# The cosine product of the rotation, made by VectorE instead of GpSimd, in a two-layer trunk on one core

## The chip, the cores and the metric

The kernel runs on one core of a Trainium2 chip. The metric is the device time of one execution in microseconds; the time before is the median of three runs. The profile is that of one further execution.

## What is computed

Two layers of a transformer trunk over 512 latent tokens (x) and 256 context tokens (ctx), width 1024, all in float32. Each layer projects the normed tokens into queries, keys and values of four groups of heads (differential, windowed, latent, grouped), attends, projects back (`w_out`), and then runs a gated feed-forward network with a short convolution. The queries and keys of the 512 latent tokens are rotated by position before they are used; this is the part that the change touches:

```
def apply_axial_rope(x, cos, sin):
    ...
    x1, x2 = xr[..., 0, :], xr[..., 1, :]
    ...
    out = jnp.stack([x1 * c - x2 * s, x2 * c + x1 * s], axis=-2)
    return out.reshape(B, S, H, d)
```

## The kernel before

Features lie on the 128 partitions, tokens along the free dimension. TensorE works in pairs of rounded floats: each float32 operand is split into a high part (ScalarE rounds it, line 249) and a low part (value minus high part, line 250, on VectorE or GpSimd), and a product is three matmuls (lines 263 to 265).

A layer has four stages. In the trace, layer 0's mixing stage lies at 55 to 470 us and layer 1's at about 1190 to 1510 us; the feed-forward network and the output projection fill the rest. In a mixing stage the kernel walks through a hand-written string of steps (`ORDER`): projections (`DQ0`, `DK0`, ...), values (`Vd`, `Vs`), heads of attention (`d0` to `d3`, `s0`, `g0`, ...), and the three steps of the latent group (`mla`). A scheduler then orders the instructions of every engine by its own estimate of their times, so that projections, softmaxes and value products of several steps interleave. When one instruction moves to another engine, the scheduler lays the whole stage out anew.

A projected tile is called `p` (or `qr` in the latent group): 128 rows by 768 tokens, of which the first 512 are rotated. The rotation (`rope`) is called 12 times a layer: ten projections, once on half a tile (64 rows), and once for `qr`. It makes two products with the sines into a scratch tile `u`, with the halves of the partitions exchanged (lines 635 and 636, 64 rows each, VectorE), one product with the cosines in place on `p` (line 642, 128 rows by 512), and a sum (line 643, VectorE). The rotated tile is split by `hilo` into `f` (ScalarE's line 249, then GpSimd's line 250), written to DRAM (`sc`, line 771) and read back by heads as an operand `op` (lines 777, 785, 792), all from SP's DMA queue, in order. The scores `s` (line 820) need that operand.

Softmax in these stages takes a maximum on VectorE (lines 828 and 834, from PSUM), the exponential on ScalarE (837), a reciprocal on VectorE (841), and a scaling on GpSimd (862, 865), with a subtraction on VectorE for the differential heads (863). The probabilities `P` are transposed on TensorE (889) into `tp`, split into `pth` (ScalarE) and `ptl` (VectorE, line 250), and multiplied with the values into `po` (896). GpSimd also makes the low parts of the weights, `wl` (line 250).

Of the kernel before, what the change touches and what calls it, by code (L numbers as in the profile page):

```python
# [14 lines left out]
ALU = mybir.AluOpType  # L15
# [7 lines left out]
S = 512  # L23
# [81 lines left out]
def _tables():  # L105
    pos = np.arange(S)
    row = (pos // 64).astype(np.float32)
    col = (pos % 64).astype(np.float32)

    def make(dim):  # L110
        n = dim // 4
        inv = (np.float32(10000.0) ** (-np.arange(n, dtype=np.float32) / np.float32(n))).astype(np.float32)
        r = np.arange(64) % (2 * n)
        a, i = r // n, r % n
        ang = np.where(a[:, None] == 0, row[None], col[None]).astype(np.float32) * inv[i][:, None]
        c, s = np.cos(ang).astype(np.float32), np.sin(ang).astype(np.float32)
        return np.concatenate([c, c], 0), np.concatenate([s, -s], 0)

    c64, s64 = make(64)
    c32, s32 = make(32)  # L120
    rope = np.ascontiguousarray(np.stack([c64, s64, c32, s32], 1))
    m = np.full((P, 7, P), NEG, np.float32)
    q = np.arange(P)[:, None]
    k = np.arange(P)[None]
    m[:, 3] = 0.0
    m[:, 2] = np.where(k >= q, 0.0, NEG)
    m[:, 4] = np.where(k <= q, 0.0, NEG)
    mask = np.ascontiguousarray(m[:, 1:6]).reshape(P, 5 * P)
    sel = np.zeros((P, 4), np.float32)
    r = np.arange(P)  # L130
    for h in range(2):
        sel[:, h] = (r % 64) // 32 == h
        sel[:, 2 + h] = r // 64 == h
    return rope, mask, sel
# [101 lines left out]
class Prog:  # L236
# [393 lines left out]
    def rope(self, p, tab, mp, rows=None):  # L630
        nc = self.nc
        ct, st = (self.ropet[:, 0], self.ropet[:, 1]) if tab == 64 else (self.ropet[:, 2], self.ropet[:, 3])
        u = self.mq.tile([P, T], F32, tag="u", bufs=1, name="u")[:, :S]
        if rows is None:
            nc.vector.tensor_tensor(out=u[0:64], in0=p[64:128, :S], in1=st[64:128], op=ALU.mult)
            nc.vector.tensor_tensor(out=u[64:128], in0=p[0:64, :S], in1=st[0:64], op=ALU.mult)
            a, b = 0, 128
        else:
            nc.vector.tensor_tensor(out=u[64:96], in0=p[96:128, :S], in1=st[96:128], op=ALU.mult)
            nc.vector.scalar_tensor_tensor(out=u[96:128], in0=p[64:96, :S], scalar=-1.0, in1=st[64:96], op0=ALU.mult, op1=ALU.mult)  # L640
            a, b = 64, 128
        nc.gpsimd.tensor_tensor(out=p[a:b, :S], in0=p[a:b, :S], in1=ct[a:b], op=ALU.mult)
        nc.vector.tensor_tensor(out=p[a:b, :S], in0=p[a:b, :S], in1=u[a:b], op=ALU.add)

    def hilo(self, p, n, mp, a=0, b=P):
# [656 lines left out]
```

## Time and profile before

| what | value |
|---|---|
| median of three runs | 1975.7 us (1970.12 to 1979.73) |
| profiled execution, its own time | 1973.07 us |
| span in its trace | 1971.3 us |
| PE busy | 1805.3 us, 92% of the span |
| DVE busy | 1135.2 us, 58% |
| ACT busy | 905.0 us, 46% |
| POOL busy | 838.5 us, 43% |

PE is TensorE's matmuls, DVE is VectorE, ACT is ScalarE, POOL is GpSimd, SP the engine that issues the DMAs. Busy shares are averages over stages that differ; the rows further down take the mixing stages apart. In a timeline row the first number is the start, the second the time it took, and the bracket at the end gives how long the engine sat idle before it and which instruction ended that.

### The profile page before, as it was taken

To read this page: it belongs to the slowest core of one execution; us is meant where nothing else is said; L and a number is where in the kernel's file an instruction comes from. 1 tells how busy PE (TensorE), PEld (TensorE's weight loads), DVE (VectorE), ACT (ScalarE), POOL (GpSimd) and SP (SyncE) were. 2 spreads that over 40 slices of the span, in tenths; PEclk is the share of its full clock that TensorE was granted. 3 is DMA by queue.
4 is the path that set the end of the run, shared out by engine and by line. 5 is a ranking of instruction groups with operands and counts; after the bars stand their busy time and mean duration, and the time that the engine had idled before them with its cause. 6 is when DMAs were issued, how large, how long until landed. Compare 5 with 4: busy or idle time off the path is not lost. (4 is left out here: it accounts for less than half of the span.)

```text
span 1971.3 us, 26510 instructions
## 1 busy us (share of the span) xinstructions
PE 1805.3 (92%) x9834; PEld 1530.0 (78%) x9834; DVE 1135.2 (58%) x2119; ACT 905.0 (46%) x1597; POOL 838.5 (43%) x559
## 2 busy tenths in 40 slices
PE   6889899898988899999999977888899899999997
PEld 3878778776877788888888866777777788888885
DVE  5466877875769755454432675776786632323235
ACT  5455567875542323231313363554787444333332
POOL 1363534543234334242424434544454145545553
PEclk8999899999998999999999998989999989999999
DMA  8663452544345324242312136524253323222322
GB/s 313 185 191 108 113 172 84 174 110 148 112 173 190 118 75 161 85 150 107 118 43 86 53 130 156 128 65 119 65 150 118 119 86 98 96 96 96 107 86 85
DMA packets 76160, 239.97 MB, mean 122 GB/s; under 512 B 11136, under 2 KB 12672, under 8 KB 73216
## 3 DMA queue, kind: packets, MB, share of 16 engines
q1 hardware_dynamic: 76032, 238.28, 38.5%
q8 instruction: 78, 1.28, 0.3%
q14 instruction: 50, 0.41, 0.1%
HBM read 201.94 MB, written 36.31 MB: 121 GB/s over the span
## 5 line engine op out<-in xcount | busy, mean ns | idle before, releaser
L250 POOL TENSOR_TENSOR wl<-wr,wh 128x1024 fp32r<-128x1024 f32 (+1 forms) x178 | 440.2, 2482 | 499.7 <-ACT wh L249 478.6
L249 ACT ACTIVATE wh<-wr 128x1024 fp32r<-128x1024 f32 (+1 forms) x186 | 193.2, 1049 | 383.7 <-PE up L264 182.5
L1222 DVE SCALAR_TENSOR_TENSOR ut<-up,pc,ut 128x769 f32<-128x769 f32 (+1 forms) x84 | 74.1, 883 | 333.6 <-ACT ut L1221 333.6
L263 PE MATMUL up<-hx,wh 128*128 128x512 f32 x672 | 262.8, 391 | 0.0
L264 PE MATMUL up<-hx,wh 128*128 128x512 f32 x672 | 262.5, 391 | 0.0
L265 PE MATMUL up<-hx,wl 128*128 128x512 f32 x672 | 262.2, 390 | 0.0
L820 PE MATMUL s<-op 128*128 128x256 f32 (+4 forms) x648 | 160.2, 358 | 34.2 <-ACT P L837 18.3
L250 DVE TENSOR_TENSOR ptl<-tp,pth 128x512 fp32r<-128x512 f32 (+1 forms) x208 | 136.2, 663 | 40.7 <-ACT pth L249 39.6
L820 PEld LDWEIGHTS s<-op 128*128 128x128 f32 (+1 forms) x648 | 110.8, 198 | 56.8 <-ACT P L837 28.3
L265 PEld LDWEIGHTS up<-hx,wl 128*128 128x128 f32 x672 | 126.4, 188 | 27.1
L263 PEld LDWEIGHTS up<-hx,wh 128*128 128x128 f32 x672 | 126.5, 188 | 25.6
L264 PEld LDWEIGHTS up<-hx,wh 128*128 128x128 f32 x672 | 126.5, 188 | 25.1
L1127 PE MATMUL dn<-wh,gh 128*128 128x512 f32 x440 | 140.3, 398 | 4.6 <-ACT gh L249 4.2
L865 POOL TENSOR_SCALAR P<-P,st 128x768 f32<-128x768 f32 (+2 forms) x120 | 95.9, 801 | 114.1 <-DVE st L841 84.5
L1127 PE MATMUL dn<-wl,gh 128*128 128x512 f32 x440 | 139.3, 396 | 0.0
L889 PE MATMUL tp<-ident,P 128*128 128x128 f32 x800 | 127.9, 280 | 12.2 <-DVE P L863 6.8
L1127 PE MATMUL dn<-wh,gl 128*128 128x512 f32 x440 | 138.0, 398 | 0.0
L249 ACT ACTIVATE pth<-tp 128x512 fp32r<-128x512 f32 (+1 forms) x208 | 116.6, 576 | 38.2 <-PE tp L889 36.7
L837 ACT ACTIVATE P<-s,st 128x768 f32<-128x768 f32 (+2 forms) x120 | 94.1, 786 | 79.2 <-DVE st L828 35.0
L497 DVE SCALAR_TENSOR_TENSOR wm<-wm,cb 128x1024 f32<-128x1024 f32 x56 | 107.1, 1925 | 31.4 <-DMA wm<-wmod 31.1
L828 DVE TENSOR_REDUCE st<-s 128x1 f32<-128x768 f32 (+2 forms) x120 | 95.6, 808 | 50.7 <-PE s L820 49.7
L896 PE MATMUL po<-ptl,vt 128*128 128x256 f32 x400 | 112.3, 303 | 13.2 <-DVE ptl L250 13.2
(286 smaller groups left out, 4326.5 us busy)
## 6 DMA issues: line engine op xcount, KB each, us to landing
wr<-wup SPq DMA_DIRECT2D x88, 512.0 KB, 3.8
wm<-wmod SPq DMA_DIRECT2D x56, 512.0 KB, 5.0
wr<-wdn SPq DMA_DIRECT2D x44, 512.0 KB, 3.8
op<-sc SPq DMA_DIRECT2D x36, 384.0 KB, 5.4
wr<-win SPq DMA_DIRECT2D x26, 512.0 KB, 4.3
wk<-wmk SPq DMA_DIRECT2D x12, 1024.0 KB, 6.9
op<-sc SPq DMA_DIRECT2D x60, 192.0 KB, 5.6
wm<-wm SPq DMA_DIRECT2D x8, 1024.0 KB, 9.4
```

The source lines that it names most:

```text
L249: self.nc.scalar.activation(out=hi, in_=src, func=AF.Copy)
L250: eng.tensor_tensor(out=lo, in0=src, in1=hi.bitcast(F32), op=ALU.subtract)
L263: mm(ps, lh, rh, start=first, stop=False)
L264: mm(ps, lh, rl, start=False, stop=False)
L265: mm(ps, ll, rh, start=False, stop=last)
L497: nc.vector.scalar_tensor_tensor(out=j, in0=raw, scalar=1.0, in1=cb[v], op0=ALU.mult, op1=ALU.mult, accum_out=self.mods[l][:, ch, f, v:v + 1])
L820: nc.tensor.matmul(full[:, o:o + w], q[:rows, qcol:qcol + P], k[:rows, c0:c0 + w], start=i == 0, stop=i == len(passes) - 1 and not msk)
L828: nc.vector.tensor_reduce(out=nm, in_=ps[:, :nk], axis=AX.X, op=ALU.max, negate=True)
L865: nc.gpsimd.tensor_scalar(out=a[:, :nk], in0=a[:, :nk], scalar1=ra, scalar2=1.0, op0=ALU.mult, op1=ALU.mult)
L889: nc.tensor.transpose(tp[:, a * 256 + j * P:a * 256 + (j + 1) * P], ptile[j][:, pos[kt]:pos[kt] + P], self.ident)
L896: nc.tensor.matmul(po[:, :256], vw, t[:, a * 256:(a + 1) * 256], start=n == 0, stop=n == total - 1)
L1127: mm(ps[:, c], a, b[:, c], start=first and i == 0, stop=last and i == 2)
```

## The change

The product with the cosines is issued to VectorE's queue, where the other three instructions of the rotation stand.

```
             a, b = 64, 128
-        nc.gpsimd.tensor_tensor(out=p[a:b, :S], in0=p[a:b, :S], in1=ct[a:b], op=ALU.mult)
+        nc.vector.tensor_tensor(out=p[a:b, :S], in0=p[a:b, :S], in1=ct[a:b], op=ALU.mult)
         nc.vector.tensor_tensor(out=p[a:b, :S], in0=p[a:b, :S], in1=u[a:b], op=ALU.add)
```

The scheduler's order changes on every engine in both mixing stages. On VectorE, at the start of layer 0's mixing stage (the rotation of `DQ0`; `wl` is the low part of a weight tile), a piece of the difference:

```order
 L635 TENSOR_TENSOR u<-p,ropet 64x512
 L636 TENSOR_TENSOR u<-p,ropet 64x512
+L642 TENSOR_TENSOR p<-p,ropet 128x512
 L250 TENSOR_TENSOR wl<-wr,wh 128x1024
 L643 TENSOR_TENSOR p<-p,u 128x512
```

The product now stands between the second product with the sines and the weight's low part. Of the 24 products six stand directly behind the second product with the sines (three of them the first three of layer 1); the other 18 have one to four other instructions in between.

On VectorE, later in layer 1's mixing stage, the sixth rotation of that layer (at 1259 us in the trace), before:

```order
L635 TENSOR_TENSOR u<-p,ropet 64x512
L636 TENSOR_TENSOR u<-p,ropet 64x512
L828 TENSOR_REDUCE st<-s 128x1
L841 RECIPROCAL st<-st 128x1
L250 TENSOR_TENSOR ptl<-tp,pth 128x512
L841 RECIPROCAL st<-st 128x1
L643 TENSOR_TENSOR p<-p,u 128x512
```

and of the change:

```order
L635 TENSOR_TENSOR u<-p,ropet 64x512
L636 TENSOR_TENSOR u<-p,ropet 64x512
L828 TENSOR_REDUCE st<-s 128x1 x2
L642 TENSOR_TENSOR p<-p,ropet 128x512
L250 TENSOR_TENSOR ptl<-tp,pth 128x512 x2
L841 RECIPROCAL st<-st 128x1
L643 TENSOR_TENSOR p<-p,u 128x512
```

The product now stands ahead of the low parts of the probabilities (`ptl`).

On SP's queue, at the start of layer 0's mixing stage (the writes of `DQ0`'s and `DK0`'s rotated tiles to `sc`, and the reads of the first operands):

```order
 L771 DMA sc<-f 16x2x768 x8
-L777 DMA op<-sc 32x2x768 x3
-L771 DMA sc<-f 16x2x768 x8
-L777 DMA op<-sc 32x2x768 x5
+L777 DMA op<-sc 32x2x768
+L771 DMA sc<-f 16x2x768 x8
+L777 DMA op<-sc 32x2x768 x7
 L511 DMA wk<-wmk 128x2048 x2
```

Two of the first operand's reads moved from ahead of `DK0`'s eight writes to behind them.

## Rows read from the trace of the kernel before

**Rows 1.** The page's busy times: engine, us, share of the span, instructions.
```profile
PE 1805.3 (92%) x9834; PEld 1530.0 (78%) x9834; DVE 1135.2 (58%) x2119; ACT 905.0 (46%) x1597; POOL 838.5 (43%) x559
```

**Rows 2.** Busy times by window, the two mixing stages; columns in the first line.
```profile
core 0: us, PE busy (x) PEld busy (x) DVE busy (x) ACT busy (x) POOL busy (x), PEclk, DMA share, GB/s
...
55.00:470.00 415.00, 376.23 (x2459) 326.50 (x2459) 294.83 (x655) 264.30 (x582) 196.13 (x193) 0.96 0.49 141
...
1190.00:1510.00 320.00, 274.75 (x1692) 240.83 (x1691) 229.65 (x479) 194.69 (x404) 155.01 (x137) 0.95 0.43 110
```

**Rows 3.** Waits of PE in layer 0's mixing stage: total us, times, longest.
```profile
PE s L820 <- DMA op<-sc: 2.8, 1, 2.8
```

**Rows 4.** Waits of PE in layer 1's mixing stage.
```profile
PE s L820 <- DMA op<-sc: 12.8, 3, 7.8
PE po L896 <- DVE ptl L250: 9.5, 10, 2.8
PE tp L889 <- DVE P L863: 3.7, 3, 2.7
```

**Rows 5.** Line 642: ns min/median/max; below, who waited for it, us and times.
```profile
L642 POOL TENSOR_TENSOR p<-p,ropet x22: 1260/1288/2027, 58.8 to 1377.9; 128x512 f32<-128x512 f32 x20, 64x512 f32<-64x512 f32 x2
...
  DVE p L643: 7.9, 7
```

**Rows 6.** Line 636 alone by window: length, busy us (instructions), clock, DMA.
```profile
55.00:470.00 415.00, 7.54 (x11) 0.96 0.49 141
1190.00:1510.00 320.00, 8.18 (x10) 0.95 0.43 110
```

**Rows 7.** Line 635 alone, the same windows and columns.
```profile
55.00:470.00 415.00, 10.28 (x11) 0.96 0.49 141
1190.00:1510.00 320.00, 13.69 (x10) 0.95 0.43 110
```

**Rows 8.** Timeline, a rotation at the start of layer 1's mixing stage.
```profile
1190.83 2.68 DVE L635 TENSOR_TENSOR u<-p,ropet 64x512 f32<-64x512 f32 x1 [2.25 <-ACT p L625]
1193.51 0.69 DVE L636 TENSOR_TENSOR u<-p,ropet 64x512 f32<-64x512 f32 x1
1194.35 1.29 POOL L642 TENSOR_TENSOR p<-p,ropet 128x512 f32<-128x512 f32 x1 [1.39 <-DVE u L636]
1195.67 0.69 DVE L643 TENSOR_TENSOR p<-p,u 128x512 f32<-128x512 f32 x1 [1.47 <-POOL p L642]
```

**Rows 9.** Timeline of DVE: first, largest and last beside line 642, two without it.
```profile
59.39 1.76 DVE L250 TENSOR_TENSOR wl<-wr,wh 128x1024 fp32r<-128x1024 f32 x1 [0.73 <-ACT wh L249]
...
61.68 1.21 DVE L250 TENSOR_TENSOR wl<-wr,wh 128x1024 fp32r<-128x1024 f32 x1
...
223.34 0.15 DVE L840 TENSOR_TENSOR st<-st 128x1 f32<-128x1 f32 x1
...
243.78 1.27 DVE L283 TENSOR_SCALAR rs_y<-rs_v 128x12 int32<-128x12 int32 x1
...
1378.57 0.56 DVE L840 TENSOR_TENSOR st<-st 128x1 f32<-128x1 f32 x1
```

**Rows 10.** Timeline of PE: first, largest and last wait for VectorE behind a rotation.
```profile
130.59 0.63 PE L889 MATMUL tp<-ident,P 128*128 128x128 f32 x4 [1.08 <-DVE ptl L250]
...
1335.71 0.39 PE L896 MATMUL po<-ptl,vt 128*128 128x256 f32 x1 [2.81 <-DVE ptl L250]
...
1379.52 0.39 PE L896 MATMUL po<-ptl,vt 128*128 128x256 f32 x1 [1.66 <-DVE ptl L250]
```

**Rows 11.** Timeline of SP's DMA issues and of PE, starts of both mixing stages.
```profile
70.83 3.59 SPq L771 DMA_DIRECT2D sc<-f  x8
74.46 2.32 SPq L777 DMA_DIRECT2D op<-sc  x5
...
1203.56 3.25 SPq L777 DMA_DIRECT2D op<-sc  x7
...
1213.47 0.77 PE L820 MATMUL s<-op 128*128 128x512 f32 x1 [7.84 <-DMA op<-sc]
```

**Rows 12.** Timeline of PE, a wait for an operand later in layer 1.
```profile
1347.97 0.59 PE L820 MATMUL s<-op 128*128 128x384 f32 x2 [1.39 <-DMA op<-sc]
```

## Prediction

> **What bounds the kernel now.** I began with the page's busy times: TensorE is busy for 92% of the span and no other engine for more than 58% [rows 1]. So only what lets TensorE stand still can move the time much. The change acts in the two mixing stages alone, so I next took the windows of those stages. TensorE is busy for 376.2 of 415 us in layer 0's and 274.8 of 320 us in layer 1's [rows 2]; it stands still for 38.8 and 45.2 us, 84 us in both. VectorE is busy for 294.8 of 415 us (71%) and 229.7 of 320 us (72%), GpSimd for 47% and 48%. The reader should see that work goes from an engine with more room to one with less, and that neither is the bound. The lists of what TensorE waited for name two things that a rotation can touch: operands that come late from DRAM, 2.8 us in layer 0 and 12.8 us in layer 1 [rows 3, 4], and VectorE, of which layer 1's largest entries are 9.5 us for `ptl` and 3.7 us for `P` [rows 4].
>
> **What is removed.** 24 products leave GpSimd, 1.29 us each in the median [rows 5], 31 us. GpSimd had room, so this by itself gives nothing. Two side effects do. VectorE stood idle for the product in 7 of the 24 rotations, 7.9 us in all [rows 5]. And some VectorE instructions were stretched while GpSimd made the product: a weight's low part took 1.76 us beside it and 1.21 us without it, a 128x1 sum 0.56 us and elsewhere 0.15 us, and one small scalar operation 1.27 us [rows 9]. I found eight that are clearly stretched, by 0.4 to 1.1 us, 5.4 us together (first, largest and last stand in the rows).
>
> **What is added.** 24 products on VectorE. The trace has none of this operation on VectorE, so I bound it by its neighbours in the same rotation, which have the same free length. The lower is line 636, which stands right behind another VectorE product: 7.54 + 8.18 us for 21, mean 0.75 us [rows 6], so 18.0 us for 24. The upper is line 635, which often starts while GpSimd is busy: 10.28 + 13.69 us for 21, mean 1.14 us [rows 7], so 27.4 us. I take 0.75, since every new product has the two products with the sines close ahead, as line 636 has line 635. VectorE's account over both stages is then 18.0 added, 5.4 given back in stretched instructions and 7.9 in idle time: 4.7 us more, of 735 us.
>
> **Which of it lies on the path.** I looked behind each rotation for the next wait of TensorE that VectorE ends. There are eight places (1.08 us at 130 us, 2.81 at 1335, 1.66 at 1379 are the first, the largest and the last [rows 10]), and I compared them with the new order. At two of the eight the awaited instruction now stands ahead of the product, so nothing is added. At six the product stands ahead of it, as in the sixth rotation of layer 1 shown above: 6 × 0.75 = 4.5 us more. At two of these six a stretched instruction stood on the way, 0.6 and 0.4 us, which goes: 1.0 us less. Net 3.5 us. At the other rotations TensorE has other matmuls queued that hide 0.75 us; without that cover the remaining 18 × 0.75 = 13.5 us would come on top.
>
> **The operands.** At the start of layer 1 the rotation is bare: the second product with the sines ends at 1194.20, the sum starts at 1195.67, 1.47 us later [rows 8]. With the product on VectorE in between this is about 0.75, so the tile is ready 0.7 us earlier, then the split, the writes and the reads, for which TensorE waits 7.84 us at 1213 [rows 11]. I take 0.8 us off for the two rotations ahead of it, at least 0 if the transfers and not the rotation set the pace. In layer 0 the tile is also 0.7 us earlier, but the new queue of SP puts two reads of the first operand behind `DK0`'s writes; at the old pace of five reads in 2.32 us [rows 11] they hold the awaited ones up by 2 × 0.46 = 0.9 us. I take 0. Later in layer 1 a wait of 1.39 us at 1348 [rows 12] hangs on a rotation in which `ptl` twice comes first and the product then follows in series, where GpSimd used to work beside it: 0.6 us more. Sum for operands: −0.8 + 0 + 0.6 = −0.2 us.
>
> **A rule weighed against this.** In the trace a VectorE product of 64x512 takes 2.68 us behind a busy GpSimd and 0.69 us right after [rows 8]. The Trainium skill (SBUF — State Buffer, Who interferes with whom) says that a VectorE instruction with two SBUF inputs contends with a GpSimd instruction that reads SBUF, and that whichever starts first has the shared port for its whole length. The stretched first product agrees. By that rule the new product could be held as line 635 is; that is the first rival, priced from rows below.
>
> **Sum.** 3.5 − 0.2 = 3.3 us on the profiled execution's own 1973.07 us gives 1976.4 us. That execution lies 2.6 us below the median of the three runs, 1975.7; moved by as much, the forecast is 1979 us, 0.17% slower than before. About 0.5% (9.9 us) is what a measurement of this kernel can tell from no change, so I call this no change: within 1965.8 to 1985.6 us.
>
> **Rivals.**
> *VectorE is held up (slower).* Each new product starts while GpSimd is making a low part, and takes 1.14 us; VectorE works in order, so all behind it waits. Then 27.4 − 5.4 − 7.9 = 14.1 us more if all of it reaches TensorE: 1990 us. It decides from about 70% of that (9.9 us) on. For it: 18 of the 24 products have other instructions between them and the products with the sines, so a GpSimd instruction can slip in; VectorE is at 71%. Against: TensorE waited for `ptl` and `P` only 13.2 us in layer 1 [rows 4].
> *The rotation is on the path (faster).* The step from the second product to the sum shrinks from 1.47 to 0.75, 0.72 us [rows 6, 8], and 24 × 0.72 = 17 us is the most that this can give: 1958 us. With 16 of the 24 on the path it is 11.5 us: 1964 us. It decides from 14 on. For it: the 15.6 us of waits for operands [rows 3, 4]. Against: VectorE idled for the product in only seven rotations [rows 5].
> *The new layout decides (either way).* The scheduler interleaves both stages anew, and its layouts differ by more than the terms above: TensorE stands still for 38.8 / 415 = 9.3% of one stage and 45.2 / 320 = 14.1% of the other [rows 2]. Both at 9.3% would be 15 us less (1960 us), both at 14.1% 20 us more (1996 us). Nothing in the rows gives its sign; the order of the two kernels tells which instructions change places, not how long they then wait.
>
> **How the numbers follow.** My forecast gets 0.55, of which 0.05 ends above 1985.6; VectorE held up 0.17; the rotation on the path 0.10; the new layout 0.18, of which 0.08 is slower, 0.05 faster, 0.05 within the bound. So slower 0.05 + 0.17 + 0.08 = 0.30, the same 0.50 + 0.05 = 0.55, faster 0.10 + 0.05 = 0.15. The predicted time is 1979 us. The likeliest case alone holds 1966 to 1988. The range reaches down to 1965, near the faster rival, and up to 1993, past the held-up VectorE and short of the layout's worst: about 2 in 10 stays outside.
>
> **What would show it.** In the profile after, line 642 on DVE should have a median of 0.69 to 0.75 us and a sum near 18 us; a sum of 25 us or more speaks for the first rival. VectorE's busy time in the two windows should rise by 10 to 15 us and GpSimd's fall by 31. TensorE's idle time there should be 80 to 95 us; under 70 or over 100 would mean that the layout, not the instruction, decided. The wait near 1213 should be 7 to 7.8 us. At the layer's start the step from the second product to the sum should be about 0.75 us. The forecast is wrong if the wait for operands at the starts changes by several us, or if `ptl` and `P` are awaited for 20 us or more in layer 1.

## The result, and the profile after

The change makes the kernel a little slower: median 1987.35 us (1979.01 to 1991.85, six runs) against 1972.91 us, ratio 1.0059 with a 95% interval of 1.0036 to 1.0082. Run once more beside the last experiments it gave 1.0043 (1.0026 to 1.0060). The forecast was 1979 us, +0.17%, called no change; the time lies in the range of 1965 to 1993 us, but above the 1985.6 us where I had let no change end. By the two medians the loss is 14.4 us, where 3.3 were forecast. The profiled execution took 1987.04 us (span 1985.2), 13.9 us of span more than [rows 1] belongs to.

The page's busy times after, to be read against [rows 1]:

```profile
PE 1820.0 (92%) x9834; PEld 1540.4 (78%) x9834; DVE 1149.7 (58%) x2143; ACT 903.6 (46%) x1597; POOL 814.8 (41%) x535
```

VectorE has 24 instructions and 14.5 us more, GpSimd 24 fewer and 23.7 us less. The figure to stop at is TensorE's: the same 9834 matmuls take 14.7 us longer, and that is the whole loss. TensorE did not stand still longer; it was busy longer.

To see where, I cut both traces at the same events: the first scores of layer 0, the last product with its values, the same two of layer 1. Windows of the kernel before (length, then each engine's busy time, PEclk, DMA share, GB/s, as in [rows 2]):

```profile
82.78:463.14 380.36, 347.25 (x2267) 299.93 (x2268) 281.23 (x642) 250.36 (x565) 181.74 (x185) 0.96 0.47 138
463.14:1213.47 750.33, 703.30 (x3641) 597.21 (x3640) 422.30 (x628) 254.66 (x339) 285.85 (x128) 0.98 0.36 120
1213.47:1517.32 303.85, 265.84 (x1657) 233.94 (x1658) 226.31 (x480) 190.98 (x401) 141.90 (x130) 0.95 0.40 104
```

and of the changed kernel:

```profile
83.23:465.85 382.62, 350.53 (x2267) 300.08 (x2268) 286.77 (x653) 249.15 (x564) 170.60 (x175) 0.96 0.47 137
465.85:1215.82 749.97, 703.20 (x3642) 598.79 (x3640) 421.48 (x631) 254.09 (x338) 283.87 (x124) 0.98 0.35 119
1215.82:1531.22 315.40, 278.48 (x1657) 243.70 (x1658) 235.46 (x489) 191.21 (x401) 133.16 (x121) 0.91 0.38 100
```

Layer 0's stage grew by 2.3 us, layer 1's by 11.55 us. In layer 1, length less busy time is 38.0 us before and 36.9 after: the idle time fell by 1.1 us. TensorE's busy time rose by 12.64 us for the same 1657 matmuls, and the column to its right says why: the mean granted clock fell from 0.95 to 0.91. A stretch granted 0.50 is at 1.2 GHz, one granted 1.00 at 2.4 GHz, so about 2 × 0.05 × 303.85 = 30 us were spent at 1.2 GHz before and 2 × 0.09 × 315.4 = 57 us after. The column is rounded; by the trace's own record the clock stands at 0.50 for 28.6 us before, in six stretches, and for 53.9 us after, in ten. Work done at half speed takes twice as long, so 25.3 us more of it costs 12.65 us, the whole rise in busy time.

The lines that answer to the prediction's own. Line 642, to be read against [rows 5] (ns min/median/max), with VectorE's wait for it gone:

```profile
L642 DVE TENSOR_TENSOR p<-p,ropet x22: 670/680/694, 58.9 to 1383.0; 128x512 f32<-128x512 f32 x20, 64x512 f32<-64x512 f32 x2
...
L642 DVE TENSOR_TENSOR qr<-qr,ropet x2: 681/682/682, 362.3 to 1442.2; 128x512 f32<-128x512 f32 x2
```

The rotation at the start of layer 1's stage, against [rows 8]:

```profile
1197.21 0.68 DVE L636 TENSOR_TENSOR u<-p,ropet 64x512 f32<-64x512 f32 x1
1197.93 0.69 DVE L642 TENSOR_TENSOR p<-p,ropet 128x512 f32<-128x512 f32 x1
1198.65 0.69 DVE L643 TENSOR_TENSOR p<-p,u 128x512 f32<-128x512 f32 x1
```

TensorE's waits in layer 1's mixing stage, against [rows 4], same window of 1190 to 1510 us (it leaves out the last 7 us of the stage before and the last 21 us after). One line of the kernel before that is not in [rows 4], then those of the changed kernel:

```profile
PE s L820 <- ACT P L837: 8.9, 10, 2.5
```

```profile
PE s L820 <- ACT P L837: 11.8, 10, 2.5
PE s L820 <- DMA op<-sc: 10.1, 3, 6.3
PE po L896 <- DVE ptl L250: 5.9, 8, 2.1
...
PE tp L889 <- DVE P L863: 2.3, 2, 1.8
```

Waits for operands, `ptl` and `P` fell (12.8 to 10.1, 9.5 to 5.9, 3.7 to 2.3 us); those for the exponential of line 837 rose, from 8.9 to 11.8. These lists do not show the loss.

What it looks like on the timeline. Windows of 2 us in the changed kernel, around a wait of 2.6 us for an operand, the second longest of layer 1:

```profile
1433.70:1435.70 2.00, 1.98 (x7) 0.96 (x6) 1.38 (x3) 1.53 (x5) 2.00 (x2) 1.00 1.02 208
1435.70:1437.70 2.00, 0.00 (x0) 0.00 (x0) 1.44 (x3) 0.30 (x1) 0.38 (x1) 0.81 1.05 236
1437.70:1439.70 2.00, 1.40 (x4) 1.21 (x5) 0.00 (x0) 0.00 (x0) 0.00 (x0) 0.50 1.02 409
1439.70:1441.70 2.00, 2.00 (x10) 1.81 (x9) 1.32 (x2) 0.00 (x0) 0.00 (x0) 0.50 0.08 31
1441.70:1443.70 2.00, 2.00 (x8) 1.49 (x7) 1.57 (x4) 1.35 (x3) 0.74 (x1) 0.50 0.04 8
1443.70:1445.70 2.00, 2.00 (x12) 1.41 (x12) 1.05 (x3) 0.22 (x1) 0.00 (x0) 0.98 0.00 0
```

and TensorE's row behind that wait:

```profile
1438.30 2.93 PE L820 MATMUL s<-op 128*128 128x512 f32 x8 [2.62 <-DMA op<-sc]
```

TensorE stands still for 2.62 us; the clock falls to 0.50 in that time and stays there until about 1443.7, though TensorE is then busy without a break. So the bill for this wait has a second part that no wait list shows: the work behind it runs at 1.2 GHz. The theory to test was this: the new order places its waits so that the clock falls more often. Its rival: VectorE's added work costs the time itself.

### The profile page after: what moved, and what is told of

It reads as the page before. It is cut to its first block, busy times and chain, and to the rows that moved or that the text cites. A ratio compares the mean times of both kernels' runs of the same rounds, so it can differ in the third digit from the quotient of the medians.

```text
span 1985.2 us, 26505 instructions
## 1 busy us (share of the span) xinstructions
PE 1820.0 (92%) x9834; PEld 1540.4 (78%) x9834; DVE 1149.7 (58%) x2143; ACT 903.6 (46%) x1597; POOL 814.8 (41%) x535
## 5 line engine op out<-in xcount | busy, mean ns | idle before, releaser
L889 PE MATMUL tp<-ident,P 128*128 128x128 f32 x800 | 129.5, 283 | 16.1 <-DVE P L863 6.3
```

Source lines behind the costliest of these rows:

```text
L889: nc.tensor.transpose(tp[:, a * 256 + j * P:a * 256 + (j + 1) * P], ptile[j][:, pos[kt]:pos[kt] + P], self.ident)
```

## The experiments

An order can be held: the scheduler takes edges that fix issue order without a wait, and instructions have the same names in both kernels. This piece, called at the end of the program, chains each engine's instructions in the order recorded from one kernel. It is shortened: `recorded` and `<NoSync>` stand for longer expressions. In the traces of the held kernels TensorE's matmuls of both mixing stages (2267 and 1657) stand in the recorded order without an exception.

```
+    for i in recorded:
+        if i.engine in last:
+            tc.add_manual_dep(i, last[i.engine], <NoSync>, reason="pinned")
+        last[i.engine] = i.name
```

| label | product on | order | extra matmuls | median us | ratio to before (95%) | median clock |
|---|---|---|---|---|---|---|
| (before) | GpSimd | old | – | 1973.53 | 1 | 0.962 |
| (the change) | VectorE | new | – | 1987.35 | 1.0059 (1.0036 to 1.0082) | 0.955 |
| dve_old_order | VectorE | old | – | 1982.39 | 1.0038 (1.0020 to 1.0056) | 0.959 |
| pool_new_order | GpSimd | new | – | 1988.86 | 1.0078 (1.0051 to 1.0104) | 0.955 |
| layer0_only | mixed | free | – | 1980.54 | 1.0041 (1.0021 to 1.0060) | 0.958 |
| layer1_only | mixed | free | – | 1983.68 | 1.0046 (1.0029 to 1.0064) | 0.957 |
| new_mask | VectorE | a third | – | 1978.20 | 1.0017 (1.0001 to 1.0033) | 0.961 |
| old_mask | GpSimd | a fourth | – | 1973.12 | 0.9989 (0.9973 to 1.0005) | 0.9635 |
| new_filled | VectorE | new | 49 | 1975.46 | 0.9999 (0.9983 to 1.0015) | 0.9665 |
| pool_new_filled | GpSimd | new | 49 | 1979.34 | 1.0023 (1.0009 to 1.0036) | 0.9645 |
| old_filled | GpSimd | old | 50 | 1971.10 | 0.9970 (0.9955 to 0.9985) | 0.9665 |
| dve_old_filled | VectorE | old | 50 | 1972.50 | 0.9980 (0.9963 to 0.9997) | 0.968 |
| new_filled3 | VectorE | new | 10 | 1983.36 | 1.0035 (1.0016 to 1.0053) | 0.958 |
| new_again | VectorE | new | – | 1983.55 | 1.0043 (1.0026 to 1.0060) | 0.958 |

The row of before is that of the first four experiments (1974.8 and 1974.9 us in the others). Each ratio was taken against the runs of before made beside it; it differs by up to 0.14% from the quotient of the medians. The last column is the median over a kernel's runs of TensorE's mean granted clock.

**Product and order, apart.** The changed line in the old order, and the old line in the new order.

> The product with the cosines is on VectorE, as in the change, but every engine's instructions are held in the order that the kernel before has (the 24 products take their places of the old global order in VectorE's queue). If the new order costs the time: the product alone costs what the prediction's sum says, about +3 us, 0.1 to 0.3% over the kernel before, and TensorE's granted clock in layer 1's mixing stage stays at about 0.94 to 0.95, its busy time there near 263 us. If the product on VectorE itself costs the time (VectorE in order, everything behind it late): +10 to +15 us, 0.5 to 0.8% over before, with the idle time of TensorE up.

> The reverse: the product stays on GpSimd, as before, but every engine's instructions are held in the order of the changed kernel. If the new order costs the time: +8 to +14 us over the kernel before, with a granted clock near 0.91 in layer 1's mixing stage and TensorE busy there for about 275 us, though no rotation has changed. If the product on VectorE costs it: 0 to +4 us, clock about 0.94 there.

The new order with no rotation changed is 0.78% slower, as slow as the change or slower: the order alone is enough. The product on VectorE in the old order costs 0.38%, 7.5 us (4 to 11). That lies between the two expectations, +3 and +10 to +15, and its interval reaches both, so the product's own cost is not settled here; it may be as large as half of the change's loss or more. The two costs do not add up: together they would be 1.16%, and the change has 0.59 or 0.43%.

What the four kernels share is TensorE's idle time, span less busy time: 166.0 us before and 165.2 with the change, 164.7 in dve_old_order and 164.4 in pool_new_order. The last two from their pages, to be read against [rows 1], in spans of 1976.0 and 1981.6 us:

```profile
PE 1811.3 (92%) x9834; PEld 1535.7 (78%) x9834; DVE 1145.7 (58%) x2143; ACT 905.2 (46%) x1597; POOL 805.7 (41%) x535
```

```profile
PE 1817.2 (92%) x9834; PEld 1537.5 (78%) x9834; DVE 1138.2 (57%) x2119; ACT 904.0 (46%) x1597; POOL 839.4 (42%) x559
```

In none of the nine profiled executions without extra matmuls is the idle time above that of the kernel before (157.3 to 166.0 us). So VectorE's added work did not cost its time as idle time of TensorE, as the rival had it: with the product as with the order, what grew is the busy time of the same 9834 matmuls.

Three of TensorE's waits for `ptl` in layer 1 show the product; the first of them in the kernel before, and all three with the product on VectorE:

```profile
1263.51 0.38 PE L896 MATMUL po<-ptl,vt 128*128 128x256 f32 x1 [1.44 <-DVE ptl L250]
```

```profile
1265.86 0.39 PE L896 MATMUL po<-ptl,vt 128*128 128x256 f32 x1 [2.23 <-DVE ptl L250]
...
1339.52 0.44 PE L896 MATMUL po<-ptl,vt 128*128 128x256 f32 x1 [2.85 <-DVE ptl L250]
...
1382.93 0.39 PE L896 MATMUL po<-ptl,vt 128*128 128x256 f32 x1 [2.09 <-DVE ptl L250]
```

Against 1.44 here and 2.81 and 1.66 in [rows 10] that is 0.79, 0.04 and 0.43 us more: up to about one product per place, as the prediction had it. One place in layer 0 lost far more, 1.08 us in [rows 10] and 3.52 us here. TensorE's row, VectorE's row ahead of it, GpSimd's beside it, and the same VectorE instruction before:

```profile
134.53 0.84 PE L889 MATMUL tp<-ident,P 128*128 128x128 f32 x4 [3.52 <-DVE ptl L250]
```

```profile
131.21 2.58 DVE L863 SCALAR_TENSOR_TENSOR P<-P,st 128x256 f32<-128x256 f32 x1
```

```profile
131.16 2.35 POOL L250 TENSOR_TENSOR wl<-wr,wh 128x1024 fp32r<-128x1024 f32 x1
```

```profile
129.35 0.49 DVE L863 SCALAR_TENSOR_TENSOR P<-P,st 128x256 f32<-128x256 f32 x1
```

A VectorE subtraction that starts 0.05 us behind a GpSimd low part ends 0.28 us after it and takes 2.58 us instead of 0.49. In the kernel before, GpSimd's low part starts 0.31 us behind the subtraction (at 129.66 us), after a wait of 0.34 us for ScalarE; here it starts first. Why the two moved against each other was not taken apart.

**Layers, apart.** The edit chooses the engine by layer:

```
+        (nc.gpsimd if self.l else nc.vector).tensor_tensor(out=p[a:b, :S], in0=p[a:b, :S], in1=ct[a:b], op=ALU.mult)
```

and the reverse for layer1_only. TensorE's order in each layer's stage is then that of the kernel with the same engine there, exactly in layer 0 and nearly in layer 1 (1653 of 1657 matmuls in common in layer0_only, 1486 in layer1_only).

> The product is on VectorE in layer 0 and on GpSimd in layer 1; the scheduler is free. Layer 0's mixing stage then has the order of the changed kernel, layer 1's that of the kernel before. From the two traces, layer 0's part of the loss is 2.2 us: if place and order matter as they do in those traces, +2 us (0 to +5), and layer 1's stage is as before (clock 0.94 to 0.95). If the loss comes evenly with the 24 products: +7 us.

> The product is on GpSimd in layer 0 and on VectorE in layer 1. From the two traces, layer 1 carries 10 to 12 of the 14 us: +10 us (8 to 13) over the kernel before, with a clock near 0.91 in layer 1's mixing stage. If the loss comes evenly with the 24 products: +7 us.

By the ratios layer 0 costs 8 us (4 to 12) and layer 1 costs 9 us (6 to 13). My expectation for layer 0, +2 from one pair of traces, was a miss: a single pair cannot size so small a part. The other expectation of both runs, +7 us each because the loss comes evenly with the products, fits both results, so these two runs do not tell the theories apart. Layer 1's stage in further executions of the new order with the product on VectorE (layer1_only, then new_again) and of the old kernel's (layer0_only):

```profile
1211.03:1528.06 317.03, 280.38 (x1657) 246.20 (x1658) 234.60 (x489) 191.48 (x401) 131.70 (x121) 0.90 0.38 100
```

```profile
1211.28:1523.52 312.24, 274.97 (x1657) 240.40 (x1658) 235.79 (x489) 191.34 (x401) 133.41 (x121) 0.93 0.39 103
```

```profile
1215.60:1516.96 301.36, 263.82 (x1657) 232.08 (x1658) 225.69 (x480) 191.03 (x401) 142.25 (x130) 0.96 0.40 106
```

So layer 1 repeats what the first pair showed: 0.90, 0.91 and 0.93 against 0.95 and 0.96, with 37 to 38 us idle each time. The two held kernels do not; layer 1's stage in pool_new_order, then in dve_old_order:

```profile
1220.93:1525.77 304.84, 268.50 (x1657) 235.68 (x1658) 229.37 (x480) 190.91 (x401) 142.70 (x130) 0.95 0.39 104
```

```profile
1214.41:1521.49 307.08, 267.65 (x1657) 235.46 (x1658) 231.74 (x489) 191.10 (x401) 130.72 (x121) 0.95 0.40 104
```

For pool_new_order a clock near 0.91 and about 275 us of busy time had been expected here, so in this stage the expectation failed; its profiled execution lost in layer 0's stage instead (86.35 to 473.32 us, 386.97 us, clock 0.95), and dve_old_order's did too (387.70 us, clock 0.95). By the trace's record of the clock, layer 1's stage spends 31.8 and 33.1 us at 1.2 GHz in these two kernels, against 24.0 and 28.6 us with the old order and GpSimd's product and 46.0, 53.9 and 61.0 us with the new order and VectorE's. So the large loss in layer 1 is shown for the new order and the product on VectorE together, and for neither alone, from one execution of each held kernel (that of pool_new_order is the fastest of its six).

**Other orders.** The step that casts the mask is moved by one place in both layers' lists, which changes no work:

```
-         "DQ0 Vd DK0 DK1 GQ0 mask Vs DQ1 SQ1 d0 SK ..."
+         "DQ0 Vd DK0 DK1 mask GQ0 Vs DQ1 SQ1 d0 SK ..."
```

> Another order with the same work: the product on VectorE as in the change, and the step that casts the mask (GpSimd) stands one place earlier in each layer's list of steps, which makes the scheduler lay layer 1's mixing stage out anew. If the order decides through the clock, with a sign that is a matter of luck: anywhere from 1975 to 1995 us, and as the granted clock goes. If VectorE's product costs it whatever the order: 1987 us within 3.

> The kernel before (product on GpSimd) with the same step moved; its order changes in few places (some 170 lines of TensorE's list, against some 2500 for the change). If the order decides: 1968 to 1985 us. If only the product's engine counts: 1973 us within 3.

With VectorE's product in this third order the kernel is only 0.17% slower than before, 5 to 8 us faster than the change in its own order (by the two ratios of the change). old_mask fitted both expectations.

**The waits filled.** If the clock behind the waits is the cost, keeping TensorE at work during them must give it back. Matmuls whose results nobody reads go into waits that recur in the traces, each batch a little shorter than its wait, with the order held (shortened):

```
+    def fill(self, line, out, may=True):
+        n = FILL.get((line, self.at[line]), 0)
+        ...
+        for _ in range(n):
+            self.nc.tensor.matmul(out, self.ident, self.ropet[:, 0, :out.shape[1]], ...)
```

It is called ahead of the matmuls of lines 820, 889 and 896 and writes into the bank that they are about to write, or a half of it that they don't use.

> The changed kernel in its own order, with 49 extra matmuls whose results nobody reads, put into 13 waits of TensorE of 0.9 to 6.3 us in the two mixing stages that the traces of the same order show again and again (some 15 to 19 us of extra work, each a little shorter than its wait). Nothing else moves. If the lower granted clock behind such waits is what the change lost: the mean granted clock rises from about 0.955 to 0.965 or more, TensorE's other matmuls take less time at 1.2 GHz, and the time falls by 8 to 15 us, to 1972 to 1979 us (0 to 0.3% over before). If what counts is the work and the waits themselves, and the clock only goes with them: 1987 us as the changed kernel, or up to 5 us more, since the extra matmuls stand in the way.

> The kernel before, in its own order, with 48 such extra matmuls in 13 of its recurring waits of 1.1 to 7.8 us (some 15 to 19 us). If the clock behind the waits costs time in the kernel before as well: 8 to 15 us less, 1958 to 1966 us, 0.4 to 0.8% faster than before. If not: 1973 us, up to 5 us more.

(The old order has 50 of them, not 48 as the text above and one below say.) In new_filled the extra matmuls keep TensorE busy for 7.88 us in layer 0 and 14.13 us in layer 1 (more than the 15 to 19 us expected), and yet the kernel is 0.4 to 0.6% faster than the change: level with before. The place shown above, in new_filled:

```profile
1421.00:1423.00 2.00, 2.00 (x8) 1.02 (x7) 1.43 (x4) 1.46 (x3) 2.00 (x2) 1.00 1.03 213
1423.00:1425.00 2.00, 1.32 (x4) 0.25 (x2) 1.33 (x2) 0.00 (x0) 0.01 (x1) 1.00 1.04 289
1425.00:1427.00 2.00, 1.88 (x12) 1.71 (x13) 0.81 (x1) 0.00 (x0) 0.00 (x0) 1.00 0.87 345
1427.00:1429.00 2.00, 2.00 (x12) 1.27 (x10) 2.00 (x4) 1.24 (x3) 0.91 (x1) 1.00 0.00 1
```

```profile
1422.44 1.88 PE L1310 MATMUL s<-ropet,ident 128*128 128x512 f32 x4
1425.12 1.66 PE L820 MATMUL s<-op 128*128 128x512 f32 x8 [0.80 <-DMA op<-sc]
```

The operand comes no earlier (1.88 + 0.80 = 2.68 us of wait against 2.62), but the clock stays at 1.00, and the same eight matmuls take 1.66 us instead of 2.93. This is the direct evidence that the clock behind a wait costs time. Over layer 1's stage:

```profile
1208.15:1515.88 307.73, 274.04 (x1705) 239.64 (x1706) 236.20 (x489) 191.08 (x401) 133.55 (x121) 0.96 0.38 104
```

0.96 instead of 0.91, and 48 records more (two for each extra matmul) in 7.7 us less. The kernel before gains too, 0.30% (0.19% by the medians), less than the 0.4 to 0.8 expected.

> The product on GpSimd, every instruction in the order of the changed kernel (as in the run that was 15 us over before), with the 49 extra matmuls in the 13 waits of that order. If the new order's cost is the granted clock behind its waits: 10 us or more of the 15 go, to 1972 to 1979 us (within 0.3% of before), mean clock 0.965 or more. If the new order has costs of its own (operands later, engines waiting): 1984 us or more.

> The product on VectorE, every instruction in the order of the kernel before, with the 48 extra matmuls of that order. The kernel before with the same extra matmuls took 0.997 of before, 1971 us. If the product's own cost is what the prediction's sum says, 3.3 us, and the rest of the 7.5 us measured in the old order was clock: 1973 to 1976 us, 0.998 to 1.001. If VectorE's product itself costs 7 us whatever the clock: 1978 us or more, 1.002 or more.

> The changed kernel in its own order with only the 10 extra matmuls of the three longest waits for operands (3 at 83 us, 5 at 1216, 2 at 1438; about 8.5 us). If every filled wait gives back its share through the clock: about half of what all 13 gave (12 us), so 1979 to 1983 us. If the short waits for VectorE's results are what brings the clock down: 1985 us or more.

> The changed kernel once more, unaltered, on the same chip as the three others, so that they can be set against it: 1983 to 1989 us, 0.4 to 0.7% over before, mean clock 0.953 to 0.958.

The new order with GpSimd's product gives back 0.55% of its 0.78%, a little past the upper edge of what the clock theory expected (1972 to 1979 us), and stays 0.23% slower than before. The old order with VectorE's product gives back 0.58%, and is then 0.10% above old_filled (each set against its own runs of before), some 2 us. With the three longest waits for operands alone filled, nothing measurable came back (1.0035 against 1.0043 beside it); that run fell between its two expectations. Its trace shows the place above repaired all the same (the eight matmuls take 1.66 us again), so a repaired place is not yet a faster kernel. The other ten waits matter, but which of them was not taken apart.

Since the old order gains from filled waits as well, the fair comparison is filled with filled. Against old_filled (0.9970) the new order is still 0.29% slower with VectorE's product and 0.53% with GpSimd's, each figure good to some 0.2%, at mean clocks of 0.9665 and 0.9645 against 0.9665. Without extra matmuls the same two differences to the old order were 0.43 to 0.59% and 0.78%. So filling the waits shows that the clock behind waits costs time in both orders; of the difference between the orders it takes away a part only, and what keeps the rest was not found. That the loss of the change is busy time at the lower clock rests on the windows and idle times above.

## Why the prediction was right, and where not

**What bounds the kernel.** This is the step that failed: "only what lets TensorE stand still can move the time much". Idle time over the whole span was 166.0 us before and 165.2 after; the time moved by 13.9 us all the same, through what TensorE's busy time costs. The clock column of [rows 2] (0.96 and 0.95) lay before the prediction, and it never used it. Its test, 80 to 95 us of idle time in the two windows and the layout to blame only under 70 or over 100, was therefore blind: 415 − 377.37 and 320 − 279.21 make 78.4 us, just under the band and well within 70 to 100, though the new order alone costs 0.78%.

**The product.** 0.75 us each and 18 us were forecast; 0.68 us and 8.18 + 8.19 = 16.4 us were measured. The first rival, the product held as line 635 is, falls: the 24 lie between 670 and 694 ns.

**What is given back.** 5.4 us of stretched instructions were to go. The runs with a held order can size this, since their VectorE work differs by the product's engine alone. VectorE's busy time rose by 10.5 us in the old order (1135.2 to 1145.7) for 17.0 us of products, so 6.5 us came back, and by 11.5 us in the new (1138.2 to 1149.7) for 16.4 us, so 4.9. The two pairs with extra matmuls rose by 6.6 and 14.8 us, so what came back lies between about 2 and 10 us: the term is of the right order, and single executions give no more. In the change it is hidden by the new order, which brings other stretched instructions. Line 636 took 0.75 us in the mean of 21 in [rows 6]; in the same windows after it is 0.88 us in the mean of 22:

```profile
55.00:470.00 415.00, 8.75 (x11) 0.95 0.48 140
1190.00:1510.00 320.00, 10.58 (x11) 0.91 0.42 110
```

and line 635 rose from 23.97 us [rows 7] to 24.95 for the same 21. VectorE's busy time over the whole execution rose by 14.5 us, near the upper end of 10 to 15; GpSimd's fell by 23.7 us instead of 31, but by 32.8 in the old order.

**The places on the path.** Forecast +3.5 us. With the order held, TensorE's waits ended by VectorE rose by 3.2 us in layer 0 (82 to 470 us: 13.1 to 16.3) and fell by 1.6 in layer 1 (1215 to 1520 us: 17.7 to 16.1), net 1.6. The three places shown above behave as forecast, and the net is of the right order; but 2.4 of the 3.2 us came from a held neighbour, which the sum did not have, and the fall in layer 1 was not forecast.

**The operands.** The step from the second product to the sum was forecast at 0.75 us and is 0.76 (1197.89 to 1198.65), down from 1.47. The wait near 1213 was 6.31 us, not 7 to 7.8. Since it was 7.84 and 5.48 us in two executions of the old order and 6.31, 5.16 and 4.47 in three of the new, an effect of 0.8 us could not be read from it. In layer 0 the wait is 3.28 us, against 2.83; no difference was taken.

**The sum.** 3.3 us as the product's own cost compares with 7.5 us (interval 4 to 11) in the old order and some 2 us there with the waits filled, both good to some 4 us. What was missing is the clock. That the time still fell into the range is luck as far as the sum goes: the range reached to 1993 us for the held-up VectorE and the layout's waits, and neither is what happened.

**The rivals.** "The new layout decides" came true on its slow side, with a chance of 0.08, but by another mechanism: it was priced by idle shares (9.3% and 14.1%), and those did not rise (9.1% and 12.7% in the same windows after). Shown: the order alone costs 0.78%, the loss lies in TensorE's busy time at the lower clock, and extra matmuls in the waits win time in either order. Not settled: what in the order makes the clock fall more often, why layer 1 shows it only with the product on VectorE, how much the product costs by itself, and whether any of this could have been read from the order ahead of a run.

## What to carry to other kernels

Where the profile shows a granted clock, judge a change that reorders work by busy time of the same instructions and by granted clock in windows cut at the same events, as well as by idle time: here idle time fell by 0.8 us while the kernel lost 13.9. Before blaming or praising an edit under a scheduler that lays everything out anew, hold the old order and then the new one with either version of the edit; orders with the same work differed by 0.9% here (old_mask and pool_new_order), more than the 0.38% of the edit in the old order. Waits that cannot be removed may be worth filling: unread matmuls in 13 waits made even the kernel before 0.3% faster (interval 0.15 to 0.45), the fastest version found.

## What the runs showed of the hardware

The scatter between executions of one program goes with the clock. Of the 29 runs of before in the first comparison the fastest took 1965.27 us at a mean granted clock of 0.968, and the slowest, 1983.60 us, had 0.957; over all of them time and clock correlate at −0.88. Kernels line up in the same way: median time times median clock is 1973.53 × 0.962 = 1898.5 for before, 1987.35 × 0.955 = 1897.9 for the change and 1988.86 × 0.955 = 1899.4 for pool_new_order; over all kernels without extra matmuls it lies between 1897.4 and 1901.1, while their times differ by 0.8%.

A VectorE instruction with both inputs in SBUF that starts just behind a GpSimd low part lasts until that has ended (2.58 us instead of 0.49, above). The Trainium skill (SBUF — State Buffer, Who interferes with whom) says that such an instruction contends with one of GpSimd that reads SBUF, and that the port they share is locked by one at a time; the trace agrees. Without GpSimd's product VectorE's other instructions took about 2 to 10 us less, over the pairs with the same order; the remaining low parts still met VectorE instructions, as here.
